# Narrower first sums, held-back weights and transposes in the adaLN modulation of norm 1, in a two-stream trunk layer on one core

## The chip, the cores and the metric

The kernel runs on 1 of the 8 cores of one Trainium2 chip. The metric is the device time of one execution in microseconds (us); lower is better. Engine names are those of the profile: PE is TensorE (the matrix engine; PEld is its weight load), DVE is VectorE, ACT is ScalarE, POOL is GpSimd, SP is SyncE, which here only issues DMAs.

## The reference

One trunk layer is computed for two groups of tokens with shared weights: 128 context tokens and 256 latent tokens, each 2048 wide. What matters here is how it begins:

```python
def modulation(cond, w_mod, b_mod):
    m = jax.nn.silu(cond) @ w_mod + b_mod
    return jnp.split(m[..., None, :], 6, axis=-1)
...
    sh1, sc1, g1, sh2, sc2, g2 = modulation(cond, w_mod_l, b_mod_l)
    h = rms_norm(x, n1) * (1 + sc1) + sh1
    q, k, v, u = project_in(h, w_in_l, qg_l, kg_l)
```

`w_mod` has 2048 rows and 6x2048 columns. Its first two blocks of 2048 columns give the shift and the scale of norm 1, for the two conditioning vectors `c_ctx` (context tokens) and `c` (latent tokens). So nothing of the input projection (`w_in`, 2048 x 4096) can be multiplied before a part of these two matrix-vector products is done. After the projection come neighbourhood attention, a Fourier branch, gates, an output projection, and a SwiGLU feed-forward part with its own norm; they aren't touched.

## The kernel before

All matrices stay in fp32. A product is made of three (`mm3`, lines 147 to 149): each operand is split into a rounded high part H and a rest L, and H·H, H·L and L·H are added up. `split` (lines 142 to 144) makes H on ScalarE (a cast) and L on VectorE (a subtraction).

**Units.** The weights are read in load units (`units`, line 171): two k-tiles (128 rows each) by 512 columns, one DMA on SP's queue, 512 KB (256 KB where there is one k-tile). Raw units have 4 buffers, split ones 3. `next_unit` (line 208) does, in this order: it issues the split of the unit two ahead; it ticks the paced work in `behind`; it issues the load of the unit six ahead (which takes the raw buffer that the split has just freed); and it hands out the present unit. Each engine works through its own queue in the order in which the program issued it, so this is the order on SP, ScalarE and VectorE.

**Groups.** The input projection needs all 16 k-tiles of h. It is done in four groups of k-tiles (`GROUPS`: 1, 2, 4 and 9 tiles), so that it can start when the first tile of h is there. In each group the 8 column chunks are run through, and what a group gives is added to an accumulator `acc` in SBUF (lines 676 to 680). Group 0 has 8 units (1 to 8, one chunk each, 9 products with 512 columns), group 1 has 8 (9 to 16, 18 products each), group 2 has 16 (17 to 32) and group 3 has 40 (33 to 72). I call the products of unit m chunk m.

**Modulation.** `mod_sums` (line 393) makes shift and scale for n k-tiles of h at a time (`MODS`). It takes the 128·n columns of both blocks of `w_mod`, all 2048 rows, in eight steps of two row tiles (four loads of four row tiles where n is 1). One step is four matmuls (line 405), which the profile records as 8: the conditioning vectors are the 32-column stationary operand, and the four matmuls (shift or scale, even or odd row tile) stand side by side in the four 32-column strips of the array. A step's two loads have 4 buffers and are issued four steps ahead, by the step that frees the buffer (`src.more`). After the eighth step ScalarE copies the sums out (line 413, `mrow`). `mod_cols` (line 417) turns them into columns: per k-tile one matmul (line 421) with the small constant `sel`, loaded from the host, which also adds the even and odd halves; then three VectorE operations add the biases and multiply by the norm's gain. `modulate(kt)` (line 533) then makes hH and hL of one k-tile: two ScalarE activations (line 550), a cast and a subtraction; for the first tile VectorE makes the product and ScalarE rounds it (lines 543 to 547). Before that, x must have been scaled by its inverse norm (line 525, one tile per unit).

**Pacing.** `prepare` (line 568) is a generator: a step of it is one step of sums, or the selector products, or the columns, or one tile of `modulate`. While a later sum runs, its steps also carry the columns and tiles of the sum before. `Paced.tick` gives it a rate per unit (`PREP`), a starting balance per group (`DUE`), and a least balance (`least`, 1 in group 0 and 3.6 after it) below which nothing is done; whatever the balance, `while prepared[0] < ...` (line 664) forces the tiles that the unit at hand needs. In group 0 this gives 2, 1, 2, 2, 2, 1 and 2 steps in units 2 to 8. When `prepare` ends, the paced work on the other modulation rows (VectorE, lines 321 to 343) begins; its results are needed from the output projection on.

Of the kernel before, what the change touches and what calls it, by code (L numbers as in the profile page):

```python
# [19 lines left out]
P = 128  # L20
# [18 lines left out]
MODS = [(0, 1), (1, 3), (4, 3), (7, 3), (10, 3), (13, 3)]  # L39
GROUPS = [(0, 1), (1, 2), (3, 4), (7, 9)]  # L40
ORDER = [6, 7, 0, 1, 2, 3, 4, 5]
DUE = [-1.4, 0, 0, 0]
PREP = [1.75, 1.8, 1.8, 1.8]
# [58 lines left out]
def trunk_kernel(ctx: ExitStack, tc: tile.TileContext, io: dict):  # L102
# [153 lines left out]
    msc = [consts.tile([P, KT, 2], F32, tag=f"msc{i}", name=f"msc{i}") for i in range(2)]  # L256
    msh = [consts.tile([P, KT, 2], F32, tag=f"msh{i}", name=f"msh{i}") for i in range(2)]
# [8 lines left out]
    with ExitStack() as ph:  # L266
# [126 lines left out]
        def mod_sums(src, kt0, n, alloc, out):  # L393


            w, nk = n * P, depth_of(n)
            pm = at_tile()
            for k0 in range(0, KT, nk):
                _, wm = src.take()
                for kk in range(0, nk, 2):  # L400
                    for ty in range(2):
                        for par in range(2):
                            k = k0 + kk + par
                            q = 32 * (2 * ty + par)
                            nc.tensor.matmul(  # L405
                                pm[q : q + 32, :w], csz[:, k, :], wm[:, ty, kk + par, :],
                                start=k < 2, stop=k >= KT - 2, tile_position=(0, q), skip_group_check=True,
                            )
                    if kk + 2 >= nk:
                        src.more()  # L410
                    if k0 + kk + 2 >= KT:
                        rows = alloc([P, w], "mrow")
                        nc.scalar.copy(rows, pm[:, :w])
                        out.append(rows)
                    yield

        def mod_cols(kt0, n, rows):

            pt = md_tile()
            for j in range(n):  # L420
                nc.tensor.matmul(pt[:, j * 4 : j * 4 + 4], rows[:, j * P : (j + 1) * P], sel, start=True, stop=True)
            m = pt[:, : n * 4].rearrange("p (k i c) -> p k i c", i=2, c=2)
            yield


            def bc(ap):
                return ap.unsqueeze(2).to_broadcast([P, n, 2])

            nc.vector.tensor_add(msh[0][:, kt0 : kt0 + n, :], m[:, :, 0], bc(bcol[:, kt0 : kt0 + n]))
            d = msc[0][:, kt0 : kt0 + n, :]  # L430
            nc.vector.tensor_add(d, m[:, :, 1], bc(bcol[:, KT + kt0 : KT + kt0 + n]))
            nc.vector.scalar_tensor_tensor(
                out=d, in0=d, scalar=1.0, in1=bc(ng[:, 0, kt0 : kt0 + n]), op0=ALU.add, op1=ALU.mult
# [4 lines left out]
        with ExitStack() as pha:  # L438
# [30 lines left out]
            sel = consts.tile([P, 4], F32, tag="sel", name="sel")  # L469
            nc.gpsimd.dma_start(sel, io["selector"])  # L470
# [62 lines left out]
            def modulate(kt):  # L533
# [9 lines left out]
                if kt == 0:  # L543
                    for sl, sc, sh in conds:
                        nc.vector.tensor_scalar(f[:, sl], v[:, sl], sc, sh, op0=ALU.mult, op1=ALU.add)
                        nc.scalar.copy(H[:, sl], f[:, sl])  # L546
# [6 lines left out]
            sums = []  # L553
# [14 lines left out]
            def prepare():  # L568
# [4 lines left out]
                for k0, n in MODS[1:]:  # L573
# [4 lines left out]
                    while k0 == 1 and prepared[0] < 3:  # L578
# [71 lines left out]
            for gi, (k0, n) in enumerate(GROUPS):  # L650
                prep.due, prep.rate = DUE[gi], PREP[gi]
                prep.least = 3.6 if gi else 1
# [3 lines left out]
                for rate, ci in zip(CHUNKS, ORDER):  # L656
# [5 lines left out]
                    for u in range(k0, k0 + n, 2):  # L662
                        wH, wL = next_unit()
                        while prepared[0] < min(u + 2, k0 + n):
# [697 lines left out]
def _tables():  # L1362
# [14 lines left out]
    row = np.arange(P)  # L1377
    selector = np.zeros((P, 4), np.float32)
    for i in range(2):
        for cnd in range(2):  # L1380
            selector[(row // 64 == i) & (row % 32 == cnd), 2 * i + cnd] = 1.0
    return {"selector": selector, "dft_lat": lat, "dft_ctx": ctx, "dft_chan": chan, "winmask": np.concatenate([mask, mask], axis=0)}
# [28 lines left out]
```

## Time and profile before

| | us |
|---|---|
| median of 3 runs | 2045.47 |
| the runs | 2044.15, 2045.47, 2046.48 |
| the profiled execution: its span | 2046.3 |
| PE busy in it | 2023.5 |
| first product of group 0 (start) | 26.35 |
| first product of group 1 (start) | 57.95 |
| last step of norm 1's sums (start) | 154.7 |

The span runs from the first instruction to the last of one profiled execution; no other time is listed for that execution, so the span stands for it. It lies within the runs and 0.8 us above their median. In the rows, "idle" in brackets is the time in which that engine had done nothing before the instruction, with what ended it. Matmuls overlap: the next starts before the last has drained, so distances between starts tell more than durations.

### The profile page before, as it was taken

How to read it: one execution, taken by the hardware profiler on the slowest of the kernel's cores; microseconds unless marked ns; L12 is line 12 of the kernel's file. 1: busy time of each engine (PE TensorE's matmuls, PEld its weight loads, DVE VectorE, ACT ScalarE, POOL GpSimd, SP SyncE). 2: the span in 40 equal slices, each digit the busy share in tenths (PEclk: the TensorE clock that was granted, in tenths of full speed). 3: DMA queues.
4: the chain of work that ended last, by engine and by line, in shares of the span. 5: the costliest groups of instructions: out<-in, count | busy, mean ns of one | idle time of the engine just before them, and what ended most of it. 6: DMA issues, size and time to landing. Idle time of an engine off the chain costs nothing.

```text
span 2046.3 us, 27564 instructions
## 1 busy us (share of the span) xinstructions
PE 2023.5 (99%) x10986; PEld 1843.5 (90%) x10986; DVE 1260.9 (62%) x1578; ACT 741.1 (36%) x1093; POOL 43.7 (2%) x92
## 2 busy tenths in 40 slices
PE   7999999999999999999999999999999999999999
PEld 4668888999999999889998999899989998999897
DVE  4646989789988778755845454545454334333456
ACT  4433232445555443334523332322322232323222
POOL 1000000000010000010000000000000000000000
PEclk8999999999999999999999999999999999999999
DMA  9995979677775776754455555554554444444453
GB/s 309 335 343 187 321 258 324 217 232 224 231 204 177 250 253 190 247 182 144 119 174 156 153 155 156 150 157 146 160 158 138 124 130 125 132 124 124 138 161 124
DMA packets 220384, 390.46 MB, mean 191 GB/s; under 512 B 28464, under 2 KB 77632, under 8 KB 220256
## 3 DMA queue, kind: packets, MB, share of 16 engines
q1 hardware_dynamic: 213088, 382.13, 59.7%
q10 hardware_dynamic: 4672, 6.31, 0.8%
q8 instruction: 86, 1.41, 0.3%
q0 software_dynamic: 2496, 0.27, 0.1%
q14 instruction: 42, 0.34, 0.0%
HBM read 371.81 MB, written 20.51 MB: 192 GB/s over the span
## 4 chain that ended last, share of the span: by engine, by line
PE 96%; DMA 2%; DVE 1%; ACT 0%; SPq 0%; issue 0%; DVEq 0%
PE mm L147 20%; PE mm L149 19%; PE mm L148 19%; PE at L147 11%; PE at L149 11%; PE at L148 11%; PE at L405 1%; DMA wm<-in_w_mod 1%; DMA wraw<-in_w_in 1%; PE at L978 1%; PE at L957 1%; DMA xc<-in_x_prompt 1%; PE at L894 1%; DVE wl L144 0%; PE at L338 0%; PE at L1154 0%
## 5 line engine op out<-in xcount | busy, mean ns | idle before, releaser
L144 DVE TENSOR_TENSOR wl<-wraw,wh 128x1024 fp32r<-128x1024 f32 (+1 forms) x464 | 559.3, 1206 | 683.8 <-ACT wh L143 683.6
L143 ACT CAST wh<-wraw 128x1024 fp32r<-128x1024 f32 (+1 forms) x464 | 481.1, 1038 | 1086.9 <-PE at L148 273.9
L147 PE MATMUL mm<-hH,wh 128*128 128x384 f32 x1152 | 387.7, 337 | 0.0
L149 PE MATMUL mm<-hH,wl 128*128 128x384 f32 x1152 | 385.2, 334 | 0.0
L148 PE MATMUL mm<-hL,wh 128*128 128x384 f32 x1152 | 385.1, 334 | 0.0
L329 DVE SCALAR_TENSOR_TENSOR accr<-wmr,csz,accr 128x1024 f32<-128x1024 f32 x240 | 304.2, 1280 | 0.1
L147 PEld LDWEIGHTS mm<-hH,wh 128*128 128x128 f32 x1152 | 216.2, 188 | 3.7 <-issue 3.7
L148 PEld LDWEIGHTS mm<-hL,wh 128*128 128x128 f32 x1152 | 216.3, 188 | 0.0
L149 PEld LDWEIGHTS mm<-hH,wl 128*128 128x128 f32 x1152 | 216.2, 188 | 0.0
L147 PE MATMUL at<-hH,wh 128*128 128x384 f32 x640 | 213.9, 334 | 0.0
L149 PE MATMUL at<-hH,wl 128*128 128x384 f32 x640 | 213.9, 334 | 0.0
L148 PE MATMUL at<-hL,wh 128*128 128x384 f32 x640 | 213.8, 334 | 0.0
L147 PE MATMUL mm<-wh,hH 128*128 128x512 f32 x404 | 160.8, 398 | 1.9 <-ACT hH L546 1.2
L148 PE MATMUL mm<-wl,hH 128*128 128x512 f32 x404 | 158.2, 392 | 0.8 <-DVE wl L144 0.8
L149 PE MATMUL mm<-wh,hL 128*128 128x512 f32 x404 | 158.5, 392 | 0.4 <-DVE hL L144 0.4
L147 PE MATMUL mm<-wh,cH 128*128 128x512 f32 x352 | 137.0, 389 | 0.0
L149 PE MATMUL mm<-wh,cL 128*128 128x512 f32 x352 | 137.0, 389 | 0.0
L148 PE MATMUL mm<-wl,cH 128*128 128x512 f32 x352 | 137.0, 389 | 0.0
L147 PEld LDWEIGHTS at<-hH,wh 128*128 128x128 f32 x640 | 120.1, 188 | 1.0 <-ACT wh L143 0.8
L148 PEld LDWEIGHTS at<-hL,wh 128*128 128x128 f32 x640 | 120.1, 188 | 0.2
L149 PEld LDWEIGHTS at<-hH,wl 128*128 128x128 f32 x640 | 120.1, 188 | 0.0
L147 PEld LDWEIGHTS mm<-wh,hH 128*128 128x128 f32 x404 | 76.2, 189 | 26.1 <-issue 4.4
(284 smaller groups left out, 2627.9 us busy)
## 6 DMA issues: line engine op xcount, KB each, us to landing
wraw<-in_w_gate_up SPq DMA_DIRECT2D x176, 512.0 KB, 3.7
wmr<-in_w_mod SPq DMA_DIRECT2D x128, 512.0 KB, 5.0
wraw<-in_w_down SPq DMA_DIRECT2D x88, 512.0 KB, 3.7
wraw<-in_w_gate SPq DMA_DIRECT2D x64, 512.0 KB, 4.6
wm<-in_w_mod SPq DMA_DIRECT2D x80, 384.0 KB, 6.8
wraw<-in_w_in SPq DMA_DIRECT2D x56, 512.0 KB, 5.9
wraw<-in_w_o SPq DMA_DIRECT2D x32, 512.0 KB, 4.7
wraw<-in_w_fnet_proj SPq DMA_DIRECT2D x16, 512.0 KB, 4.8
```

The costliest lines, as they stand in the source:

```text
L143: nc.scalar.copy(H, x)
L144: nc.vector.tensor_sub(L, x, fr(H))
L147: nc.tensor.matmul(out, aH, bH, start=start, stop=False)
L148: nc.tensor.matmul(out, aH, bL, start=False, stop=False)
L149: nc.tensor.matmul(out, aL, bH, start=False, stop=stop)
L329: nc.vector.scalar_tensor_tensor(out=acc[:, cnd], in0=wm, scalar=sc, in1=acc[:, cnd], op0=ALU.mult, op1=ALU.add)
L405: nc.tensor.matmul(pm[q : q + 32, :w], csz[:, k, :], wm[:, ty, kk + par, :], start=k < 2, stop=k >= KT - 2, tile_position=(0, q), skip_gro ...
L894: nc.tensor.matmul(po[j][:, cols], qx[rows[j], q], kx[rows[j], k], start=i == 0, stop=i == 2, tile_position=(j * HD, 0),)
L957: nc.tensor.transpose(o[:, i * P : (i + 1) * P], sc[:, j, c0 : c0 + P], ident)
L978: nc.tensor.matmul(po[j][:, CTX:TOK].rearrange("p (t q) -> p t q", t=2), w[1 + kc], x.rearrange("p (t b) q -> p t b q", t=2)[:, :, 2 * kc ...
```

## The change

- `MODS`: the sums are made for 1, 2, 2, 2, 3, 3 and 3 k-tiles, not for 1, 3, 3, 3, 3 and 3. After the second and the fourth sum, `prepare` finishes the columns and tiles at once (`k0 + n in (3, 7)`); before, it did so after the second, up to tile 2.
- Of the second sum, the steps of its last half no longer issue the loads that are due (the first four of the third sum). They are kept in `owed` and issued in the first unit of group 1, after `next_unit`.
- In group 1 the preparation has the balance -2, the rate 2.9 and the least balance 1.
- `mod_cols` uses transposes in place of the selector products, and adds the even and odd halves in a second VectorE add, for shift and scale together; three VectorE operations as before. For all sums but the first, an empty step stands ahead of the transposes. The selector and its load go.
- For the first tile VectorE writes hH itself, and ScalarE makes the unrounded product `f` from which hL is taken.

```diff
-MODS = [(0, 1), (1, 3), (4, 3), (7, 3), (10, 3), (13, 3)]
+MODS = [(0, 1), (1, 2), (3, 2), (5, 2), (7, 3), (10, 3), (13, 3)]
 GROUPS = [(0, 1), (1, 2), (3, 4), (7, 9)]
 ORDER = [6, 7, 0, 1, 2, 3, 4, 5]
-DUE = [-1.4, 0, 0, 0]
-PREP = [1.75, 1.8, 1.8, 1.8]
+DUE = [-1.4, -2, 0, 0]
+PREP = [1.75, 2.9, 1.8, 1.8]
...
-    msc = [consts.tile([P, KT, 2], F32, tag=f"msc{i}", name=f"msc{i}") for i in range(2)]
-    msh = [consts.tile([P, KT, 2], F32, tag=f"msh{i}", name=f"msh{i}") for i in range(2)]
+    ms1 = consts.tile([P, KT, 2, 2], F32, tag="ms1", name="ms1")
+    msh, msc = (
+        [ms1[:, :, i], consts.tile([P, KT, 2], F32, tag=f"ms2{i}", name=f"ms2{i}")] for i in range(2)
+    )
...
                     if kk + 2 >= nk:
-                        src.more()
+                        if kt0 == 1 and k0 >= KT // 2:
+                            owed.append(src.more)
+                        else:
+                            src.more()
...
         def mod_cols(kt0, n, rows):
 
+            if kt0:
+                yield
             pt = md_tile()
             for j in range(n):
-                nc.tensor.matmul(pt[:, j * 4 : j * 4 + 4], rows[:, j * P : (j + 1) * P], sel, start=True, stop=True)
-            m = pt[:, : n * 4].rearrange("p (k i c) -> p k i c", i=2, c=2)
+                nc.tensor.transpose(pt[:, j * P : (j + 1) * P], rows[:, j * P : (j + 1) * P], ident)
+            m = pt[:, : n * P].rearrange("p (k i a c) -> p k i a c", i=2, a=2, c=32)
             yield
...
-            nc.vector.tensor_add(msh[0][:, kt0 : kt0 + n, :], m[:, :, 0], bc(bcol[:, kt0 : kt0 + n]))
-            d = msc[0][:, kt0 : kt0 + n, :]
-            nc.vector.tensor_add(d, m[:, :, 1], bc(bcol[:, KT + kt0 : KT + kt0 + n]))
+            some = slice(kt0, kt0 + n)
+            b = bcol.rearrange("p (i k) -> p k i", i=2)[:, some].unsqueeze(3).to_broadcast([P, n, 2, 2])
+            d = ms1[:, some]
+            nc.vector.tensor_add(d, m[:, :, :, 0, 0:2], b)
+            nc.vector.tensor_add(d, d, m[:, :, :, 1, 0:2])
             nc.vector.scalar_tensor_tensor(
-                out=d, in0=d, scalar=1.0, in1=bc(ng[:, 0, kt0 : kt0 + n]), op0=ALU.add, op1=ALU.mult
+                out=msc[0][:, some], in0=msc[0][:, some], scalar=1.0,
+                in1=ng[:, 0, some].unsqueeze(2).to_broadcast([P, n, 2]), op0=ALU.add, op1=ALU.mult,
             )
             yield
...
-            sel = consts.tile([P, 4], F32, tag="sel", name="sel")
-            nc.gpsimd.dma_start(sel, io["selector"])
...
                 if kt == 0:
                     for sl, sc, sh in conds:
-                        nc.vector.tensor_scalar(f[:, sl], v[:, sl], sc, sh, op0=ALU.mult, op1=ALU.add)
-                        nc.scalar.copy(H[:, sl], f[:, sl])
+                        nc.vector.tensor_scalar(H[:, sl], v[:, sl], sc, sh, op0=ALU.mult, op1=ALU.add)
+                        nc.scalar.activation(out=f[:, sl], in_=v[:, sl], func=AF.Identity, scale=sc, bias=sh)
                     nc.vector.tensor_sub(L, f, fr(H))
                     return
...
-            sums = []
+            sums, owed = [], []
...
                     follow = columns_and_tokens(k0, n)
-                    while k0 == 1 and prepared[0] < 3:
+                    while k0 + n in (3, 7) and prepared[0] < k0 + n:
                         yield next(follow)
...
-                prep.least = 3.6 if gi else 1
+                prep.least = 3.6 if gi > 1 else 1
...
                         wH, wL = next_unit()
+                        while gi and owed:
+                            owed.pop()()
                         while prepared[0] < min(u + 2, k0 + n):
                             prep.step()
```

More of the change, by code (lines that the diff above doesn't have):

```diff
@@ L417, in mod_cols @@
         def mod_cols(kt0, n, rows):
+            if kt0:
+                yield
             pt = md_tile()
             for j in range(n):
-                nc.tensor.matmul(pt[:, j * 4 : j * 4 + 4], rows[:, j * P : (j + 1) * P], sel, start=True, stop=True)
-            m = pt[:, : n * 4].rearrange("p (k i c) -> p k i c", i=2, c=2)
+                nc.tensor.transpose(pt[:, j * P : (j + 1) * P], rows[:, j * P : (j + 1) * P], ident)
+            m = pt[:, : n * P].rearrange("p (k i a c) -> p k i a c", i=2, a=2, c=32)
             yield
-            def bc(ap):
-                return ap.unsqueeze(2).to_broadcast([P, n, 2])
-            nc.vector.tensor_add(msh[0][:, kt0 : kt0 + n, :], m[:, :, 0], bc(bcol[:, kt0 : kt0 + n]))
-            d = msc[0][:, kt0 : kt0 + n, :]
-            nc.vector.tensor_add(d, m[:, :, 1], bc(bcol[:, KT + kt0 : KT + kt0 + n]))
+            some = slice(kt0, kt0 + n)
[3 more added lines that the diff above has]
+            nc.vector.tensor_add(d, d, m[:, :, :, 1, 0:2])
             nc.vector.scalar_tensor_tensor(
-                out=d, in0=d, scalar=1.0, in1=bc(ng[:, 0, kt0 : kt0 + n]), op0=ALU.add, op1=ALU.mult
+                out=msc[0][:, some], in0=msc[0][:, some], scalar=1.0,
+                in1=ng[:, 0, some].unsqueeze(2).to_broadcast([P, n, 2]), op0=ALU.add, op1=ALU.mult,
             )
@@ L1376, in _tables @@
     mask = np.where(inside, 0.0, -1e30).astype(np.float32)
[L1377 to L1382, printed above, removed]
+    return {"dft_lat": lat, "dft_ctx": ctx, "dft_chan": chan, "winmask": np.concatenate([mask, mask], axis=0)}
 _INS = [
```

## The prediction

> **What bounds the kernel now.** I read the page first, then busy time by stage, then the instructions of the first 66 us in order. The page's first line and its chain:
>
> ```profile
> span 2046.3 us, 27564 instructions
> ...
> PE 96%; DMA 2%; DVE 1%; ACT 0%; SPq 0%; issue 0%; DVEq 0%
> ```
>
> By stage (length, then busy us of PE, PEld, DVE, ACT and POOL, granted clock, DMA share, GB/s):
>
> ```profile
> 26.35:57.24 30.89, 29.75 (x142) 16.69 (x142) 14.99 (x27) 15.90 (x27) 0.00 (x0) 0.90 1.05 367
> ...
> 165.00:2046.30 1881.30, 1874.18 (x10100) 1742.61 (x10098) 1172.19 (x1429) 672.03 (x973) 37.14 (x75) 1.00 0.58 180
> ```
>
> From 165 us on TensorE is busy but for 7 us, and nothing there is edited: whatever the change does is done before, and moves the end one for one. Busy time hides waits in the first stage, because a matmul that waits for data is drawn long, so I read starts. TensorE from the first product of group 0 to the second unit of group 1:
>
> ```profile
> 26.35 0.80 PE L147 MATMUL mm<-wh,hH 128*128 128x512 f32 x1 [1.23 <-ACT hH L546]
> ...
> 30.66 2.44 PE L405 MATMUL at<-wm,csz 128*32 128x384 f32 x16
> ...
> 33.03 0.50 PE L147 MATMUL mm<-wh,hH 128*128 128x512 f32 x1
> ...
> 38.35 1.82 PE L405 MATMUL at<-wm,csz 128*32 128x384 f32 x12
> ...
> 41.15 0.50 PE L147 MATMUL mm<-wh,hH 128*128 128x512 f32 x1
> ...
> 43.42 1.64 PE L405 MATMUL at<-wm,csz 128*32 128x384 f32 x12
> ...
> 46.04 0.50 PE L147 MATMUL mm<-wh,hH 128*128 128x512 f32 x1
> ...
> 48.32 1.28 PE L405 MATMUL at<-wm,csz 128*32 128x384 f32 x8
> ...
> 50.87 0.48 PE L147 MATMUL mm<-wh,hH 128*128 128x512 f32 x1
> ...
> 57.95 0.50 PE L147 MATMUL mm<-wh,hH 128*128 128x512 f32 x1 [0.71 <-ACT hH L143]
> ...
> 63.17 2.14 PE L405 MATMUL at<-wm,csz 128*32 128x384 f32 x24
> 65.24 0.50 PE L147 MATMUL mm<-wh,hH 128*128 128x512 f32 x1
> ```
>
> The chain of waits shows the same kinds of work where nothing is late:
>
> ```profile
> 73.71 2.72 PE at L405 x32
> ...
> 86.33 0.83 PE at L421 x6
> 87.16 0.78 PE at L405 x8
> ```
>
> A step of the sums is 8 records: four take 2.72, so 0.68 each, and one alone 0.78, so a burst costs 0.10 more. The gaps between the chunks of group 0 are 33.03-30.66 = 2.37 (two steps, low clock), 0.78 (one), 41.15-38.35 = 2.80 and 46.04-43.42 = 2.62 (two each, 1.46 if nothing were late), and 50.87-48.32 = 2.55 (one, and the selector products): 11.1. Some 3 us of that is waiting for modulation weights, on a queue that is full (share 1.05).
>
> **Stage A, group 0.** A 256-column step is two thirds, 0.45. The gaps become 1.9, 0.55, 1.0, 1.0 and 0.55, and 0.35 for two transposes one unit later: 5.35, if the weights are there. Rows of 1.5 and 2 KB run at 376 GB/s, and of 512 bytes, in the stretch that is mostly theirs, at 246:
>
> ```profile
> 15.00:20.00 5.00, 3.70 (x19) 2.71 (x16) 4.17 (x11) 3.87 (x11) 0.00 (x0) 0.66 0.93 246
> ...
> 35.00:50.00 15.00, 14.04 (x77) 6.17 (x75) 7.00 (x12) 6.66 (x12) 0.00 (x0) 1.00 1.06 376
> ```
>
> So a transfer of 256 KB in rows of 1 KB takes 0.70 to 1.07, against 1.05 for 384 KB now. I take 0.75, nearer to the wide rows, as the slow stretch isn't full. The last step's data then come 15x0.3 = 4.5 us sooner than now (about 48.8, inside the burst of 48.32), at 44.3, and are wanted at 44.2. Gain 5.7; at 1.07 about 2.7. Chunk 8, which ends at 57.95-0.71 = 57.24, would end at 51.5.
>
> The first tile gains nothing that lasts:
>
> ```profile
> 25.62 0.67 DVE L545 TENSOR_SCALAR hf<-xT,msc,msh 128x128 f32<-128x128 f32 x2
> ...
> 26.76 0.56 DVE L547 TENSOR_TENSOR hL<-hf,hH 128x384 fp32r<-128x384 f32 x1 [0.47 <-ACT hH L546]
> ```
>
> Its first product may start 0.2 to 0.4 sooner, since VectorE writes hH itself; but the third needs hL, which now waits for two ScalarE activations (0.99 together in a row below) from 25.7 on: 26.7, as before. I book 0, at most 0.4. The selector's load was one of several small ones on POOL's queue, none in the chain: 0.
>
> **Stage B, the start of group 1: a new wait.** Group 0 has room for 12 steps, now 8 sums, the empty one, transposes, columns, tile 1. So transposes move from unit 6 to 7, columns from 7 to 8, and tile 2 from 8 to 9. ScalarE and VectorE work in order, and in unit 8 the columns stand behind the split of unit 10, whose cast waits until chunk 7 has freed its buffer. The same order stands in the trace at chunk 20:
>
> ```profile
> 118.65 1.05 ACT L143 CAST wh<-wraw 128x1024 fp32r<-128x1024 f32 x1 [3.02 <-DMA wraw<-in_w_in]
> ...
> 122.35 0.52 ACT L143 CAST hH<-hf 128x384 fp32r<-128x384 f32 x1
> ```
>
> From cast to finished hH: 122.87-118.65 = 4.2. Unit 8 adds a scaling (0.5) and the dependence of the second add (0.1): 4.8. Chunk 7 ends at 49.45, so tile 1 is ready at 54.25, and TensorE waits 2.8 after chunk 8, not 0.71. For tile 2, ScalarE's rows at that border, and VectorE's:
>
> ```profile
> 57.38 0.51 ACT L143 CAST hH<-hf 128x384 fp32r<-128x384 f32 x1
> 57.80 0.99 ACT L550 ACTIVATE hf<-xT,msh,msc 128x128 f32<-128x128 f32 x2
> 58.82 0.51 ACT L143 CAST hH<-hf 128x384 fp32r<-128x384 f32 x1
> 59.23 1.07 ACT L676 COPY acc<-mm 128x512 f32<-128x512 f32 x2
> 60.19 1.06 ACT L143 CAST wh<-wraw 128x1024 fp32r<-128x1024 f32 x1
> ```
>
> ```profile
> 57.98 0.55 DVE L525 TENSOR_TENSOR xT<-xT,rB 128x384 f32<-128x384 f32 x1
> ...
> 61.29 1.23 DVE L144 TENSOR_TENSOR wl<-wraw,wh 128x1024 fp32r<-128x1024 f32 x1 [0.76 <-ACT wh L143]
> ```
>
> Tile 2 now follows tile 1 by 58.82-57.38 = 1.44. Afterwards two accumulator copies and the cast of unit 11 (0.96 each, by starts) come between: 3.4, so 57.65. TensorE has three products to do meanwhile (0.85), waits 2.5, and 0.3 for hL. Chunk 9 ends at 57.7+0.3+15x0.227 = 61.4, 9.9 us after chunk 8, against 63.17-57.24 = 5.9. Loss 4.0.
>
> **Stage C, the held weights.** Unit 9 issues four held loads (eight transfers) behind the load of unit 15 on SP's queue, and that one waits for the split of unit 11, whose raw buffer it takes. Today, SP's row and the two loads' sizes and times to landing:
>
> ```profile
> 62.54 0.37 SPq L187 DMA_DIRECT2D wraw<-in_w_in  x1
> ```
>
> ```profile
> wraw<-in_w_in SPq DMA_DIRECT2D x1, 512.0 KB, 3.7
> ```
>
> ```profile
> wm<-in_w_mod SPq DMA_DIRECT2D x1, 384.0 KB, 4.5
> ```
>
> The split ends at 62.52 and the load goes out at 62.54. Afterwards it ends at 53.75+0.42+0.96+1.06+0.03+1.23 = 57.45; unit 15 lands at 61.15, and pairs of 0.75 at 62.65, 64.15 and 65.65. But unit 10 begins with three steps (due -2+2x2.9 = 3.8), and TensorE is there at 61.4. Chunk 10 starts at 65.65+0.55 = 66.2, 4.8 after chunk 9, against 65.24-63.17 = 2.07. Loss 2.7. SP's own issues don't bound it (0.37 each, two for a pair of 1.5), nor does their number, which grows by 16. From below: with everything landed 1.46, a gain of 0.6. From above: 1.5 more, if the first pair takes the lone load's 4.5 twice over.
>
> **Stage D, the rest of group 1.** Gaps now 2.72, about 3.1 (three steps, selector products) and 2.72: 8.5. Afterwards 4x1.46, 0.55, two sets of transposes 0.7, and 1.0 in unit 15, where step, empty step and transposes come in one go behind a cast of 1.05: 8.1. The queue needs 6x0.75+1.4 = 5.9 a unit, TensorE 4.1+1.46 = 5.6: 0.8 late over the units. Net +0.4. At 1.07 a transfer it would be 7.8 a unit, up to 11 us over five units, of which I take a quarter into the forecast's own range.
>
> **Stage E, group 2.** By the end of group 1 today's bursts (24, 32, 24 and 32 records) hold 14 steps, 6 of them of the third sum; afterwards none, so 6x0.68 and two bursts are paid here: +4.3. Nine tiles' selector products (0.83 for three) become transposes:
>
> ```profile
> 10.57 0.49 PE L494 MATMUL at<-ident,xc 128*128 128x128 f32 x3
> ```
>
> Three take 0.49 with the last one's drain, so -1.2 here with the handover (0 to -1.5). By the Trainium skill's TensorE: Matmul & The Clock Gate, Part 4, a transpose is about 275 ns in a kernel; by that three would take 0.83 and the sum would be 1.2 higher. The row decides here. In unit 16 the columns and tiles 5 and 6 stand ahead of chunk 16's accumulator adds, which take as long as this copy:
>
> ```profile
> 53.20 0.69 DVE L678 COPY acc<-mm 128x512 f32<-128x512 f32 x1 [2.96 <-PE mm L149]
> ```
>
> By the rows above the last hL ends 3.7+0.42+1.02+0.51+0.6 = 6.2 us after the unit's cast, the first add at 6.9; chunk 17's second set of products wants that bank 4.1+1.4 = 5.5 us after it. So +1.4, say +1.5, as nothing else lies between. Counting steps, the preparation ends in unit 34, not 30, and the modulation rows start four units later; their third kind then ends in the last unit of the output projection, whose 4 us of products cover its last steps: 0, or 1 if not.
>
> Sum: -5.7+4.0+2.7+0.4+4.3-1.2+1.5 = **+6.0**. On the profiled span that is 2052.3; the span lies 0.8 above the median of the runs and within them, so the forecast is 2045.5+6.0 = **2051.5**; its own range is 2047.5 (faster transfers, the first pair 2 us earlier, 0.4 in the first tile) to 2055 (a quarter of stage D's bound, 1 for the late rows).
>
> **Rivals.** *The held weights come in time*: stage C costs 1.46, not 4.8, so +2.7, 2048.2. For it: the queue is otherwise empty then. Against it: SP's order, above.
>
> *Not slower: ScalarE and VectorE run ahead.* B and C both hang on the cast of unit 10 waiting for chunk 7. If the columns come right after the transposes, tile 1 is ready before chunk 8 ends, the split of unit 11 is done 4 us sooner, and the loads with it: -4.0-3.3, and with D's 1.0 and E's 1.5 up to -9.8, so -1.3 to -3.8, 2044.2 to 2041.7. It decides if hH of tile 1 ends before 51.5. For it: both engines are half idle in group 0 (15 to 16 of 30.89). Against it, the longest wait of ScalarE in the first 150 us (total, times, longest), which is the wait of those casts for a chunk to end:
>
> ```profile
> ACT wh L143 <- PE mm L149: 46.2, 13, 6.1
> ```
>
> *The clock drops.* From the end of chunk 8 to tile 2 (51.5 to 57.7) TensorE would wait 5.3 of 6.2 us. The trace has a case of what that does:
>
> ```profile
> 20.00:25.00 5.00, 3.06 (x69) 2.38 (x69) 2.58 (x8) 1.26 (x3) 0.00 (x0) 1.00 0.81 252
> 25.00:30.00 5.00, 3.77 (x10) 2.68 (x10) 2.53 (x9) 1.98 (x5) 0.00 (x0) 0.58 0.97 310
> ```
>
> After a stretch with 3.06 of 5 busy the clock falls to 0.58. Half speed for some 4 to 7 us costs 2 to 3.4: +8 to +9.4, 2053.5 to 2055. The Trainium skill's TensorE: Matmul & The Clock Gate, Part 1, says the same of an idle window of about 3.4 us, and that the window runs free; by that it would come in some runs only.
>
> **How the numbers follow.** Forecast 0.50, weights in time 0.17, engines ahead 0.18, clock 0.15. A difference of 0.2% (4.1 us) is about what can be told from none. Faster by more: the lower part of engines ahead and what I overlook in stage A, 0.10. Within: its rest 0.08, weights in time 0.17, and the forecast's lower end 0.10: 0.35. Slower: the rest, 0.55. The range, 2044 to 2055.5, takes in the forecast's bounds (0.45), weights in time, half of engines ahead and most of the clock (0.10): 0.8.
>
> **What would show it.** Right: chunk 8 ends near 51.5, tile 1's hH near 54 with TensorE idle 2 to 3 us ahead of it and again ahead of tile 2; the first sums of unit 10 wait on weights for 3 us; L405 has 24 steps after group 1. Wrong: chunk 9 starts within 1 us of chunk 8's end, or the burst of unit 10 takes under 2 us.

## The result and the profile after

The changed kernel takes 2058.68 us (median of 4 runs, 2053.18 to 2060.18), the kernel before beside it 2045.02 (4 runs): a ratio of 1.006, interval 1.0046 to 1.0075. It is slower by 0.6%, 13 us, about twice the 6.0 that I forecast and above the range. The page's first line and its chain of waits:

```profile
span 2058.4 us, 27683 instructions
PE 68%; DVE 1%; issue 0%; ACTq 0%; ACT 0%
```

The shares add up to 69%, because this chain is followed back only to 638.89 us; it says nothing of the stages ahead of that, where nearly all of the loss lies. TensorE is still the busy engine, with 2028.6 of 2058.4 us (99%, as before).

This execution took 2060.18 us, so 1.8 lie around the span. That corrects a step of the prediction: the profiled execution of before, with its span of 2046.3, took some 2048.1, 2.6 above the median and not 0.8. Part of its 12.1 us distance to the changed kernel's is chance.

TensorE from the first product of group 0 to unit 10 (start, duration, what it is, idle before it; line 405 of before is 407 here, 421 is 428):

```profile
24.85 0.50 PE L147 MATMUL mm<-wh,hH 128*128 128x512 f32 x1 [1.02 <-DVE hH L548]
...
26.08 0.58 PE L149 MATMUL mm<-wh,hL 128*128 128x512 f32 x1 [0.50 <-DVE hL L550]
...
44.84 0.38 PE L428 MATMUL at<-ident,mrow 128*128 128x128 f32 x2
44.98 0.48 PE L147 MATMUL mm<-wh,hH 128*128 128x512 f32 x1
...
48.96 0.39 PE L149 MATMUL mm<-wh,hL 128*128 128x512 f32 x1
52.22 0.50 PE L147 MATMUL mm<-wh,hH 128*128 128x512 f32 x1 [2.87 <-ACT hH L143]
...
55.56 0.80 PE L147 MATMUL mm<-wh,hH 128*128 128x512 f32 x1 [2.25 <-ACT hH L143]
...
60.00 0.62 PE L148 MATMUL mm<-wl,hH 128*128 128x512 f32 x1
60.42 0.43 PE L149 MATMUL mm<-wh,hL 128*128 128x512 f32 x1
...
61.48 0.64 PE L407 MATMUL at<-wm,csz 128*32 128x256 f32 x8
62.50 1.33 PE L407 MATMUL at<-wm,csz 128*32 128x256 f32 x8 [0.39 <-DMA wm<-in_w_mod]
64.06 1.25 PE L407 MATMUL at<-wm,csz 128*32 128x256 f32 x8 [0.23 <-DMA wm<-in_w_mod]
65.25 0.50 PE L147 MATMUL mm<-wh,hH 128*128 128x512 f32 x1
```

Chunk 8 ends at 49.35. The two waits that were forecast at the border are there, with 2.87 (2.8) and 2.25 (2.5), for tiles 1 and 2. But after the second the products start 0.42 to 0.43 apart, where 0.23 is usual: the granted clock has fallen (last column but two below), in the rival's way:

```profile
50.00:55.00 5.00, 1.09 (x3) 0.48 (x3) 2.57 (x7) 4.30 (x9) 0.00 (x0) 0.87 0.43 133
55.00:60.00 5.00, 4.44 (x11) 3.40 (x11) 2.16 (x5) 0.51 (x1) 0.00 (x0) 0.50 0.70 217
```

So the border from the end of chunk 8 to the burst of unit 10 takes 61.48-49.35 = 12.1, not 9.9.

The part that I had not seen lies 300 us later, in the gate stage, which the change doesn't edit. ScalarE, TensorE, and then SP's queue there:

```profile
371.41 1.06 ACT L143 CAST wh<-wraw 128x1024 fp32r<-128x1024 f32 x1
375.98 0.83 ACT L143 CAST uH<-fraw 128x768 fp32r<-128x768 f32 x1 [3.51 <-DMA fraw<-s_qkvu]
376.71 0.85 ACT L1038 COPY gst<-mm 128x384 f32<-128x384 f32 x2
```

```profile
377.24 0.44 PE L147 MATMUL mm<-hH,wh 128*128 128x384 f32 x1 [1.84 <-ACT gst L1038]
...
378.76 0.52 PE L147 MATMUL mm<-hH,wh 128*128 128x384 f32 x1
379.08 0.52 PE L148 MATMUL mm<-hL,wh 128*128 128x384 f32 x1
```

```profile
355.38 0.42 SPq L301 DMA_DIRECT2D wmr<-in_w_mod  x1
...
356.33 0.46 SPq L301 DMA_DIRECT2D wmr<-in_w_mod  x1
...
362.55 0.46 SPq L301 DMA_DIRECT2D wmr<-in_w_mod  x1
...
365.61 0.34 SPq L301 DMA_DIRECT2D wmr<-in_w_mod  x1
...
368.81 0.56 SPq L707 DMA_DIRECT2D fraw<-s_qkvu  x1
```

Read from the bottom: four loads of the modulation rows' weights (512 KB each) stand close ahead of the Fourier branch's input. That lands at 375.9, 7 us after its issue, and ScalarE's cast waits for it 3.51. Behind the cast, in ScalarE's order, are the copies that free the gate stage's PSUM banks, so TensorE waits 1.84, and then runs at half clock for 3.4 us (products 0.32 apart, not 0.17). In the kernel before the same load is issued at 362.16, with one load of rows in the 13 us ahead of it. Counted from the start of unit 33 (184.61 there, 191.65 here) that is the same moment, 177.6 against 177.2 us. TensorE doesn't wait there, as the second view, of the whole gate stage, shows (its columns are those of the prediction's stages):

```profile
357.60 0.46 SPq L299 DMA_DIRECT2D wmr<-in_w_mod  x1
361.29 0.37 SPq L187 DMA_DIRECT2D wraw<-in_w_gate  x1
362.16 0.56 SPq L702 DMA_DIRECT2D fraw<-s_qkvu  x1
```

```profile
340.00:384.00 44.00, 44.00 (x268) 42.91 (x267) 34.16 (x38) 17.95 (x28) 4.47 (x9) 1.00 0.88 293
```

### The profile page after: what moved, and what is told of

It reads as the page before. It is cut to its first block, busy times and chain, and to the rows that moved or that the text cites. A ratio compares the mean times of both kernels' runs of the same rounds, so it can differ in the third digit from the quotient of the medians.

```text
span 2058.4 us, 27683 instructions
## 1 busy us (share of the span) xinstructions
PE 2028.6 (99%) x11034; PEld 1848.1 (90%) x11034; DVE 1264.4 (61%) x1581; ACT 742.1 (36%) x1094; POOL 43.4 (2%) x91
## 4 chain that ended last, share of the span: by engine, by line
PE 68%; DVE 1%; issue 0%; ACTq 0%; ACT 0%
PE mm L147 13%; PE mm L148 13%; PE mm L149 13%; PE at L147 10%; PE at L149 10%; PE at L148 10%; PE at L1159 0%; PE at L340 0%; DVE wl L144 0%; PE at L983 0%; DVE aL L144 0%; DVE x L1360 0%; DVE d L1359 0%; PE at L899 0%; PE at L962 0%
```

## The experiments

My theory after the result had two parts. One: the input projection loses because the empty step puts the columns a unit late, with the waits and the clock drop at the border, and because of the held weights and the six moved steps. Two: the rest is lost behind it, because the modulation rows, which begin when the preparation ends, are later (by a count of steps in unit 34, not 30, and 54 of their steps done at the end of the input projection, not 61). Rivals: one cause alone at the border; the loss behind as chance, or from another part of the change.

The table has all kernels. Each leg is a difference of two starts of TensorE in that kernel's profiled execution: from the first product to the last of chunk 8 (before: 26.35 to 56.85), to unit 10's first product (65.24), to unit 17's (103.22), to unit 33's (184.61), to the end of the span (2046.3). "Rows" is the count of row steps done at the end of the input projection; I call it the phase of the rows, since it says which of their loads meet the stages behind. The ratio is to the kernel before beside it, whose median was 2044.6 to 2045.3 beside the experiments. Changes of the total hold all legs, so an edit is judged by the leg that it aims at.

| kernel | median us | ratio | first product | to c8 | to u10 | to u17 | to u33 | to the end | rows |
|---|---|---|---|---|---|---|---|---|---|
| before | 2045.02 | | 26.35 | 30.5 | 8.4 | 38.0 | 81.4 | 1861.7 | 61 |
| before, second trace | 2046.78 (one run) | | 25.54 | 30.8 | 8.4 | 38.0 | 81.4 | 1860.9 | 61 |
| after | 2058.68 | 1.006 (1.0046 to 1.0075) | 24.85 | 24.1 | 16.3 | 39.1 | 87.3 | 1866.7 | 54 |
| 1, no empty step | 2056.21 | 1.0054 (1.0041 to 1.0068) | 24.59 | 24.7 | 15.2 | 39.1 | 85.1 | 1863.9 | 54 |
| 2, no hold-back | 2054.85 | 1.005 (1.0038 to 1.0063) | 24.98 | 24.5 | 13.7 | 38.8 | 86.6 | 1864.3 | 54 |
| 6, neither | 2049.78 | 1.0022 (1.0014 to 1.0031) | 25.86 | 24.8 | 7.9 | 41.7 | 85.1 | 1863.1 | 54 |
| 11, neither, 5 buffers | 2050.04 | 1.0023 (1.0013 to 1.0032) | 26.16 | 24.2 | 7.9 | 38.7 | 85.1 | 1865.5 | 54 |
| 12, the same, rate 2.1 | 2046.37 | 1.0004 (0.9995 to 1.0013) | 25.77 | 24.0 | 7.9 | 38.9 | 85.9 | 1860.8 | 61 |
| 10, after, waits filled | 2058.5 | 1.0063 (1.0051 to 1.0076) | 24.90 | 24.1 | 15.4 | 39.4 | 87.0 | 1867.4 | 54 |
| 4, after, rows caught up | 2058.52 | 1.0063 (1.0051 to 1.0076) | 24.63 | 24.2 | 15.9 | 37.8 | 86.6 | 1866.3 | 62 |
| 7, after, 7 row steps less | 2054.36 | 1.0046 (1.0034 to 1.0059) | 24.66 | 24.4 | 15.8 | 38.2 | 87.2 | 1861.1 | as 61 |
| 13, after, rate 2.1 | 2069.36 | 1.0114 (1.0098 to 1.0129) | 24.74 | 24.8 | 16.0 | 39.0 | 94.2 | 1870.3 | 58 |
| 3, before, rows late | 2053.01 | 1.0037 (1.0024 to 1.0049) | 24.67 | 29.5 | 8.4 | 38.0 | 81.4 | 1869.4 | 54 |
| 8, before, transposes | 2043.58 | 0.9991 (0.9982 to 1.0) | 25.13 | 28.3 | 8.5 | 37.7 | 80.7 | 1860.5 | 61 |
| 14, the same, 5 buffers | 2043.07 | 0.9991 (0.9982 to 1.0) | 26.80 | 26.8 | 8.5 | 37.7 | 80.6 | 1860.7 | 61 |
| 9, six sums | 2050.21 | 1.0026 (1.0016 to 1.0036) | 24.69 | 25.2 | 9.1 | 47.7 | 82.5 | 1861.1 | 61 |

### The border: experiments 1, 2, 6 and 10

**1.** The empty step goes.

```diff
-            if kt0:
-                yield
             pt = md_tile()
```

> The changed kernel without the empty step ahead of the transposes; the smaller sums, the held weights, the transposes and the first tile's chain stay. My theory: 7.0 us of the loss is made by unit 33, most of it at the border of chunks 8 and 9, because the empty step puts the columns one unit later, behind the cast of unit 10. Without it the two waits there (2.87 and 2.25) shrink to under 1 together, TensorE's clock stays at full after 50 us, and the border (end of chunk 8 to the burst of unit 10) takes 6 to 7 us, not 12.1. Each later set of transposes then waits 0.3 to 1 for its copied row. By unit 33 the kernel stands +1 to +3 against the kernel before; the rows still start in unit 34, so the +5 behind the input projection stays: 2052 to 2055. Rival, the held weights make the border long: the waits stay, 2057 to 2060. Rival, the late rows have no part in it: what is won in the input projection is all, and the part behind it goes too: 2047 to 2050.

Half right. The waits at the border shrink, but a new one stands at the burst of unit 10:

```profile
50.48 0.50 PE L147 MATMUL mm<-wh,hH 128*128 128x512 f32 x1 [0.82 <-ACT hH L143]
...
59.63 0.62 PE L407 MATMUL at<-wm,csz 128*32 128x256 f32 x4 [3.89 <-DMA wm<-in_w_mod]
```

Chunk 9 is done 5.8 us sooner, at 55.7, and the burst behind it waits for the weights that were held back. After that wait the granted clock is 0.50 from 61 to 64 us, so the clock drop has only moved. The leg to unit 10 gains 1.1, and the median, 2056.21, is 1.2 above the top of what I expected.

**2.** The loads go out as their buffers come free (`owed` goes).

```diff
-                        if kt0 == 1 and k0 >= KT // 2:
-                            owed.append(src.more)
-                        else:
-                            src.more()
+                        src.more()
...
-                        while gi and owed:
-                            owed.pop()()
```

> The changed kernel with the weights of the second half of the second sum loaded in group 0 as their buffers come free, not held until unit 9. My theory: the border is long because of the empty step, so both waits there stay (2 to 3 us each); group 0 gets up to 5 us longer, since 2 MB more pass a full queue (chunk 8 ends at 51 to 54, not 49.35), and the border gets shorter by about as much, as its end hangs on chunk 7's end plus a fixed chain. Net within 2 us of the changed kernel, 2056.5 to 2060.5. Rival, the held weights are the cause of the border's waits (an issue on SP's queue stands ahead of what the columns need): the border shrinks to 6 us, and the whole to 2052 to 2054.

The two waits are those of the changed kernel to the digit, and the burst of unit 10 waits for nothing. The median is 1.65 below the bottom of what I expected. Group 0 doesn't get longer, as I had thought: the leg to chunk 8 is 24.5, 0.4 more than in the changed kernel. So the hold-back bought next to nothing in group 0; in the changed kernel the queue stands at a share of 0.54 (173 GB/s) from 45 to 50 us, and here at 1.08 (371 GB/s).

```profile
52.69 0.50 PE L147 MATMUL mm<-wh,hH 128*128 128x512 f32 x1 [2.87 <-ACT hH L143]
...
56.04 0.80 PE L147 MATMUL mm<-wh,hH 128*128 128x512 f32 x1 [2.25 <-ACT hH L143]
...
61.72 1.50 PE L407 MATMUL at<-wm,csz 128*32 128x256 f32 x24
```

**6.** Both edits together.

> The changed kernel without the empty step and without the hold-back; the seven sums, the transposes and the first tile's chain stay. Each of the two alone left a long border of chunks 8 and 9 (14 us and 13.7 us from the end of chunk 8 to the burst's first product of unit 10), for two reasons: waits for tiles 1 and 2 with the empty step, waits for the held weights without it. My theory: both have to go, and then the border takes 7 to 8 us as in the kernel before, chunk 9's neighbours gain 4 to 5 us by unit 10 against a kernel that starts its first product at the same time, and this is given back by unit 33 (the six steps of the third sum that move to group 2 cost 4.3). The rows still start in unit 34, so about +5 behind the input projection stays: 2049.5 to 2052.5. Rival, the queue is the bound in groups 0 and 1, so that the weights come late whatever their order: no better than with one of the two, 2054 to 2056.

As expected: 8.4 us of the leg to unit 10 are gone (16.3 to 7.9), where one alone brought 1.1 and the other 2.6. The two causes cover each other: whichever goes, the other is late next.

**10.** TensorE is kept busy in the two waits.

```diff
+                        first = gi == 1 and ci == ORDER[0]
                         for t in range(NT):
                             sl = slice(t * P, (t + 1) * P)
                             for kk in range(min(k0 + n - u, 2)):
+                                if first and t == 0:
+                                    for _ in range(15 - 4 * kk):
+                                        nc.tensor.matmul(po[kk][:, :TOK], hH[0][:, :P], hH[0], start=True, stop=True)
```

> The changed kernel with TensorE kept busy through the two waits at the border of chunks 8 and 9: 15 products of 384 columns ahead of tile 1's first product and 11 ahead of tile 2's, written to a bank that the next real product starts anew. My theory: the half clock from 53.66 to 60.49 comes of the two waits and costs 2.2 us of the border's 12.1; filled, the clock stays at full, the burst of unit 10 starts 9.5 to 10.3 us after the end of chunk 8, and the whole is 2 us shorter, 2056 to 2057.5. Rival, the clock has no part in it, as TensorE waits there anyway: the border stays at 12, 2058 to 2060.

The clock stays at full:

```profile
55.00:60.00 5.00, 4.39 (x19) 2.83 (x19) 3.03 (x6) 0.85 (x3) 0.00 (x0) 1.00 0.71 219
```

```profile
59.24 0.39 PE L149 MATMUL mm<-wh,hL 128*128 128x512 f32 x1
59.86 0.62 PE L407 MATMUL at<-wm,csz 128*32 128x256 f32 x4 [0.23 <-DMA wm<-in_w_mod]
60.73 0.63 PE L407 MATMUL at<-wm,csz 128*32 128x256 f32 x4 [0.24 <-DMA wm<-in_w_mod]
61.59 2.87 PE L407 MATMUL at<-wm,csz 128*32 128x256 f32 x16 [0.23 <-DMA wm<-in_w_mod]
64.39 0.50 PE L147 MATMUL mm<-wh,hH 128*128 128x512 f32 x1
```

Chunk 9 ends 10.2 us after chunk 8 (59.63 against 49.39), 2.0 sooner than in the changed kernel (61.55 against 49.35). The burst now meets the held weights and takes 59.63 to 64.39, 4.8 us in place of 3.8. So 0.9 of the 2.0 is left at unit 10: the rest of the clock drop had been hidden behind the wait for these weights. The total, 2058.5, is where the rival put it, and the last leg alone is 0.7 longer here, about what two traces of the kernel before differ by (0.8). That the two waits bring the half clock is shown; its price in the total is not.

### Behind the input projection: experiments 3, 4, 7 and 13

**3.** Only the rows of the kernel before are made later.

```diff
                 src = row_weights()
-                yield
+                for _ in range(8):
+                    yield
```

> The kernel before with the modulation rows begun seven steps later (seven empty steps at their start), and nothing else. The input projection does the same as before up to unit 30. My theory: late rows cost about 5 us in the gate stage and behind it, as their loads then run against the loads of the Fourier stage's input: 2049 to 2051, with a wait of TensorE for a PSUM bank (gst, ScalarE) near 375 us and a stretch at half clock after it. Rival, the +5 comes of something else in the change (the transposes, other buffers): 2044.5 to 2046.

The direction is right and the size larger: 2053.01, ratio 1.0037 (1.0024 to 1.0049). The legs of the input projection are those of before; the last leg is 7.7 to 8.4 longer. The wait stands where it was expected, and a second one, from the rows' own chain, at 943 us:

```profile
369.24 0.44 PE L147 MATMUL mm<-hH,wh 128*128 128x384 f32 x1 [1.88 <-ACT gst L1034]
```

```profile
944.86 0.22 PE L362 MATMUL at<-ident,colr 32*128 32x32 f32 x1 [2.22 <-DMA colr<-s_row]
```

**4.** The rows of the changed kernel catch up in group 3.

```diff
-CHUNKS = [1.8, 1.8, 1.8, 1.4, 1.4, 0.95, 0.95, 1.6]
+CHUNKS = [2.034, 2.034, 2.034, 1.582, 1.582, 1.073, 1.073, 1.808]
```

> The changed kernel with the rates of the modulation rows in the last group of the input projection 1.13 times as high, so that they have done 62 steps at its end (54 in the changed kernel, 61 in the kernel before) and go on in the gate stage as in the kernel before. My theory: the +7 by unit 33 stays, the +5 behind it goes: 2052.5 to 2055. Rival, the +5 is a chance of the clock or of another part: 2057 to 2060.

A miss, 2058.52. The wait near 375 us is gone, but at over two steps a unit TensorE reaches the rows' sums before VectorE has them ready, inside the input projection:

```profile
263.14 1.05 PE L340 MATMUL at<-accr,ones 128*32 128x512 f32 x4 [0.32 <-DVE accr L331]
265.47 1.05 PE L340 MATMUL at<-accr,ones 128*32 128x512 f32 x4 [1.28 <-DVE accr L331]
```

In the gate stage another wait stands in place of the old one: 1.34 us at 350 us for VectorE's split of a weight unit. Its last leg is no shorter (1866.3 against 1866.7). This run can't separate the phase from the density.

**7.** The rows of the changed kernel have seven steps less to do, at the old rates. It leaves out three k-tiles of one modulation row, so it serves for its time alone.

```diff
                 src = row_weights()
-                yield
...
-                for k in range(KT):
+                for k in range(3 if ty == ROWS[0] and cc == 0 else 0, KT):
                     _, wm = src.take()
...
```

> The changed kernel with seven steps of the modulation rows left out (three of the 16 k-tiles in the first half of the first kind, and the empty step at their start; so that kind's row is not the reference's). The input projection ends at the same step of the rows as in the kernel before, 61, at the same rate, so the gate stage and all behind it meet the rows in the same phase. My theory (the rows' phase costs the part behind the input projection): the wait of 1.84 near 375 us and the half clock after it go, and 4 to 5 us with them: 2053.5 to 2055.5. Rival, phase of the rows is not it (as the run with higher rates, which stayed at 2058.5, may be read): 2057.5 to 2060.

As expected: 2054.36, and the last leg is that of the kernel before (1861.1). The gate stage in the changed kernel and in this one, by the same window:

```profile
340.00:384.00 44.00, 42.16 (x242) 41.84 (x241) 36.05 (x37) 15.62 (x22) 0.00 (x0) 0.96 0.94 339
```

```profile
340.00:384.00 44.00, 44.00 (x267) 42.91 (x266) 34.14 (x41) 18.21 (x29) 4.46 (x9) 1.00 0.87 302
```

25 products more in 44 us, no idle time, full clock, as in the kernel before.

**13.** One rate of the changed kernel, so that the preparation ends sooner with nothing left out.

```diff
-PREP = [1.75, 2.9, 1.8, 1.8]
+PREP = [1.75, 2.9, 2.1, 1.8]
```

> The changed kernel with that one number alone, 2.1 in place of 1.8. My theory: nothing is gained up to unit 33 (8 to 10 us behind the kernel with late rows), the wait near 375 us and the half clock go, and the whole comes out where the kernel with seven steps left out did: 2053 to 2055.5. Rival, leaving out work was what helped there, not the phase: 2057 to 2060.

A bad miss, 2069.36, and not the test that I meant. My count of steps was for a kernel without the empty step; with it the rows stand at step 58, another phase and not that of before. And group 2 loses 7 us more, since its denser bursts outrun the queue and the clock drops after the wait:

```profile
162.44 0.84 PE L407 MATMUL at<-wm,csz 128*32 128x384 f32 x4 [1.89 <-DMA wm<-in_w_mod]
```

```profile
165.00:170.00 5.00, 5.00 (x18) 4.01 (x17) 1.38 (x2) 0.00 (x0) 0.00 (x0) 0.76 0.97 348
```

### A version without the losses: experiments 11, 12, 9, 8 and 14

**11.** Experiment 6 loses 3.8 us between units 10 and 17, as its buffers hold a third less: a step of 256 columns fills one with 512 KB. A fifth buffer, on experiment 6's kernel:

```diff
-                return wmp.tile(shape, F32, tag=name, bufs=4 if name == "wm" else 1, name=nm(name))
+                return wmp.tile(shape, F32, tag=name, bufs=5 if name == "wm" else 1, name=nm(name))
...
-            for _ in range(4):
+            for _ in range(5):
                 src.more()
```

> The kernel without the empty step and the hold-back, with five buffers for modulation weights instead of four, and five loads ahead. There the queue stood half idle from 55 to 60 us (135 GB/s), while all four buffers were full, and the bursts of units 12 and 13 then waited for it: a step of 256 columns fills a buffer with 512 KB where one of 384 columns fills it with 768. My theory: a fifth buffer brings back 1 to 2 us of the 5.2 lost between units 10 and 13: 2047.5 to 2049. Rival, the queue has no room to use it: 2049 to 2050.5.

The leg from unit 10 to 17 gains 3.1 (41.7 to 38.7), more than I expected, and the total nothing: 2050.04 is where the rival put it, but not for the rival's reason, as the queue had room. The last leg is 2.4 longer: the gain moved the collision in the gate stage to a worse place (a wait of 2.16 us there, against 0.63 in experiment 6).

**12.** The same with rate 2.1 in group 2, which here brings the rows to step 61.

> The kernel without the empty step and the hold-back and with five buffers, and the preparation's rate in group 2 at 2.1 in place of 1.8: by the count of steps the rows then start in unit 30 and stand at step 61 at the end of the input projection, as in the kernel before, and nothing is left out. In the kernel with five buffers unit 33 came at the same time as in the kernel with late rows and before's input projection (0.1 later), but 3.8 us were lost behind the input projection. My theory: those go, as the rows are in before's phase again, and the whole is 2045 to 2047. Rival, those losses come with any shift of the input projection's end against the rows' loads: 2048.5 to 2051. Rival, the denser steps of group 2 wait for the queue: 2047 to 2049, with the loss ahead of 190 us.

As expected, 2046.37, 3.7 less than 11, with the last leg of before (1860.8) and nothing left out. With 7 this shows that the phase of the rows makes the loss: of the kernels whose rows stand where they stood before, all seven traces have a last leg of 1860.5 to 1861.7; of the seven with 54 steps all have 1863.1 to 1869.4. The waits say the same. All seven with 54 steps wait in the gate stage for a copy to `gst` (0.6 to 2.2 us), and 0.7 us near 640 us for the copy of the rows' own sums; none of the other seven traces has either wait. In the changed kernel:

```profile
642.42 0.66 PE L869 MATMUL at<-ident,kp 128*128 128x128 f32 x4 [0.70 <-ACT accr L344]
```

So with the losses gone the narrower sums come out even: what group 0 wins is paid between units 17 and 33 (85.9 against 81.4).

**9.** Six sums, of 1, 2, 4, 3, 3 and 3 tiles, on experiment 6's kernel. To make room, the norm weights share a buffer with the inverse norm (`rows_n` and `rB`); the first product comes no later for it (24.69).

```diff
-MODS = [(0, 1), (1, 2), (3, 2), (5, 2), (7, 3), (10, 3), (13, 3)]
+MODS = [(0, 1), (1, 2), (3, 4), (7, 3), (10, 3), (13, 3)]
```

> Sums of 1, 2, 4, 3, 3, 3 k-tiles (six, not seven), with the transposes and the first tile's chain, without the empty step and the hold-back. By the count of steps the preparation ends in unit 30 and the rows stand at step 61 at the end of the input projection, as in the kernel before, so that the part behind it should cost nothing. My theory: group 0 keeps the 4 to 5 us that the smaller second sum gives it, some of it is paid in group 1, whose sum has 512 columns a step, 1 to 1.7 comes from the transposes: 2041.5 to 2044.5. Rival, the DMA queue is the bound through group 1, so what is won in group 0 is given back there: 2044.5 to 2046.5.

A miss, 2050.21: the last leg is right, but from unit 10 to 17 it takes 47.7, as the steps of 512 columns wait for a full queue (65 to 70 us):

```profile
66.27 1.05 PE L407 MATMUL at<-wm,csz 128*32 128x512 f32 x4 [0.26 <-DMA wm<-in_w_mod]
67.62 1.05 PE L407 MATMUL at<-wm,csz 128*32 128x512 f32 x4 [0.30 <-DMA wm<-in_w_mod]
```

```profile
65.00:70.00 5.00, 4.44 (x20) 1.54 (x19) 1.26 (x2) 0.00 (x0) 0.00 (x0) 1.00 1.05 400
```

**8.** The kernel before with the transposes alone (with their VectorE operations, and without the selector's load).

```diff
-                nc.tensor.matmul(pt[:, j * 4 : j * 4 + 4], rows[:, j * P : (j + 1) * P], sel, start=True, stop=True)
+                nc.tensor.transpose(pt[:, j * P : (j + 1) * P], rows[:, j * P : (j + 1) * P], ident)
```

> The kernel before with the transposes in place of the selector products (15 of them), their three VectorE operations, and no empty step; sums, due times and first tile as before. My theory: three transposes take 0.49 in place of 0.83, so 0.34 for each of five sums, less what a wait for the copied row takes back: 2043.6 to 2045. Rival, a transpose costs as much as a selector product here: 2045 to 2046. Rival, the transposes without the empty step wait for the row that ScalarE copies, up to 0.8 in each of five sums: 2046.5 to 2048.5.

**14.** The same with five buffers.

> The kernel before with the transposes and with five buffers for modulation weights in place of four. My theory: in groups 0 and 1 of the kernel before the queue is full or the bursts find their weights (no idle of TensorE ahead of them after 60 us), so a fifth buffer changes nothing: 2043 to 2044.5. Rival, drawn-out matmuls of the bursts hide waits for weights that the fifth buffer takes away: 2041 to 2042.5.

Both give a ratio of 0.9991 (0.9982 to 1.0): 2043.58 and 2043.07, the fastest kernels here, though the gain is at the edge of what the runs can tell. Experiment 8 is at the lower end of what I expected, and 14 as expected: the fifth buffer changes no leg behind chunk 8. The steady part of it is seen in the legs: 0.3 from unit 10 to 17 and 0.7 from 17 to 33. From chunk 2's first product to chunk 8's last these two take 21.7 and 20.5, against 23.7 to 24.2 in the three traces with before's code there; the transposes' own 0.3 doesn't explain that, and it stays open. The selector products of before and the transposes, by form (records, ns):

```profile
L421 PE MATMUL at<-sel,mrow x32: 168/253/273, 24.7 to 163.9; 128*128 128x4 f32 x32
```

```profile
L423 PE MATMUL at<-ident,mrow x16: 270/273/475, 23.3 to 159.5; 128*128 128x128 f32 x16
```

One transpose lasts no less than one pass of a selector product, but there are half as many records.

**5.** The kernel before again.

> The kernel before, unedited, for a second trace of it. My theory: the profiled execution of before that the prediction rests on was a slow one at its start (two stretches of 3.41 us in a row at half clock, 25.8 to 32.6), so that chunk 8's last product starts at 54.1 and the span is 2043 to 2044.5, as the kernel with late rows showed up to 330 us. Rival: 56.5 to 57 is usual, and that other kernel's start was luck: a span of 2045.5 to 2047.

Between the two: a span of 2045.0, with chunk 8's last product at 56.3. The legs from chunk 8 on agree with the first trace to 0.1 (the last one to 0.8). What differs between executions of one program is its start, up to the first products.

## Why the prediction was wrong

The sign and the mechanisms of the input projection were right; the size was too small, and the step that failed is the one that bounded the matter at the start: "nothing there is edited: whatever the change does is done before, and moves the end one for one", with its companion in stage E, late modulation rows at "0, or 1 if not".

- **The late rows.** I had the count right (the rows begin in unit 34, not 30) and followed only their results' due time at the output projection. I did not ask what their loads, moved by seven steps, would meet. They meet the gate stage: 5.0 us in the trace (1866.7 against 1861.7 from unit 33 on), 4.3 in the medians (2058.68 to 2054.36, experiment 7), 7.7 with nothing else changed (experiment 3).
- **At the output projection**, where I had looked for the price of late rows, the changed kernel waits for nothing of theirs; experiment 3 waits 2.22 us.
- **Stage A**: forecast -5.7, measured 24.1-30.5 = -6.4 between the two profiled executions. From chunk 2's first product to chunk 8's last it is 18.5 against 23.8, -5.3, which is what the forecast has for these gaps. Of the other 1.1, 0.5 is the forecast for the first burst; the rest is chance, as the first chunk ran partly at half clock in both (products 0.43 apart), for longer in the kernel before. The first tile gained nothing that lasts: the wait ahead of its first product went from 1.23 to 1.02, and its hL makes the third product wait 0.50. The first product itself starts at 24.6 to 26.8 in kernels with either form.
- **Stages B and C**: 9.9 and 4.8 forecast, 12.1 and 3.8 measured, together 1.2 more. With the clock held up they are 10.2 and 4.8 (experiment 10): the chain was right, and the clock-drop rival, at 0.15, happened (its price of 2 to 3.4 us was 2.0 at chunk 9's end and 0.9 at unit 10). By the Trainium skill's TensorE: Matmul & The Clock Gate, Part 1, the clock falls after an idle window of about 3.4 us, and the window runs free, so the drop would come in some runs only. Here neither wait is that long (2.87 and 2.25), and all five traces with both waits unfilled have the drop at this place (after, 2, 4, 7, 13): waits of 4.9 to 5.1 us in 6.2 brought it in five of five.
- **Stage D**: forecast +0.4, measured +1.2 (39.1 against 38.0), in experiments 4 and 7 -0.2 and 0.2; within what I allowed.
- **Stage E**: forecast 4.6, measured 5.9, and 5.2 in experiments 2 and 4. The six moved steps (of the fourth sum, which the prediction calls the third) are right: without the wait at chunk 17 the leg is 85.1 (experiments 1 and 6), 3.7 over before, where +4.3-1.2 = 3.1 was forecast. The wait of chunk 17 for its bank was forecast at 1.5 and is 1.64 in the trace. The transposes give 0.7 in group 2, not 1.2; the Trainium skill's TensorE: Matmul & The Clock Gate, Part 4, has about 275 ns for one in a kernel, and the 273 of the record here agrees. That nothing would be gained, as the prediction works out from it, does not hold: a record's length is not what it costs, as the next product starts 0.14 after the start of a pair (44.84 to 44.98).
- **The sum** by legs is -6.4+7.9+1.2+5.9+5.0 = 13.6, less the 1.5 by which the changed kernel's execution had its first product sooner: 12.1, the difference of the spans. In the medians it is 13.3 to 13.7. The forecast's 6.0 stands against the 8.6 of the first four legs: even without the late rows it would have been some 2.6 short by these traces, and 3.0 by the medians (2054.36 in experiment 7, 2045.34 beside it).

What stays open: how much a collision costs. With the same 54 steps the last leg is between 1863.1 and 1869.4; I can show where each waits, not predict which transfer it will be. The 0.9 us from experiment 10's earlier unit 10 isn't seen in the total. Of the last leg's 5.0 us the changed kernel has lost 3.7 by the first product with `chanH` (384.08 before, 394.79 after); of the other 1.4 the wait of 0.7 near 640 us is one part, and the rest is not accounted for.

## What to carry to other kernels

Work that is paced by a count of steps and issues its own loads is moved as a whole when anything ahead of it takes more steps; ask what its transfers will stand in front of in stages that the edit never touches, and read the queue there, not only the due time of its results. When a wait has two causes, taking one away shows the other: of the leg to unit 10 one edit here took 1.1 us, the other 2.6, and both 8.4. And a gain in an early stage is worth nothing until the loads behind it are seen to keep their place, as experiments 11 and 12 show.

## What was not expected of the hardware

A single wait of TensorE of some 2 us can halve the clock for 3.4 us soon after: it did after 1.84 (after, at 377 us), 1.88 (experiment 3) and 2.19 (experiment 10). It did not after 2.16 us in the same place in experiment 11: its wait, and the window around it with a clock of 1.00:

```profile
368.10 0.45 PE L147 MATMUL mm<-hH,wh 128*128 128x384 f32 x1 [2.16 <-ACT gst L1031]
```

```profile
365.00:372.00 7.00, 4.84 (x28) 4.52 (x27) 3.55 (x4) 4.35 (x7) 0.00 (x0) 1.00 0.70 191
```

So the length of a wait doesn't settle it. The idle window of about 3.4 us in the Trainium skill's TensorE: Matmul & The Clock Gate, Part 1, is longer than each of these waits, so half clock comes earlier here than that figure says. That the window runs free, as the same section of the Trainium skill has it, would fit the difference between like waits, but no run here moved a wait against the window to show it.

One program's start differs between executions. The first product of group 0 came at 26.35 and 25.54 in the two traces of before, and at 24.67 in experiment 3, which is the same program up to unit 30; the last product of chunk 8 at 56.85, 56.31 and 54.13. That is more than most single edits here are worth, and all later legs of the input projection agree to 0.1.
